# A one-core hybrid encoder layer: bank-emptying operations issued ahead of chain work, and two assumed delays shortened

## The chip, the cores and the metric

The kernel runs on one core of one Trainium2 chip. The metric is the device time of one execution in microseconds, as the median of several runs. Before the change it is 1443.79 us (three runs, 1440.97 to 1444.25). About 0.3% (4.3 us) is what a measurement of this kernel can tell from no change.

## The reference, cut to what matters

One layer, sequence 2048, width 1024, all in float32. A normalised input is projected by one matrix into three head groups; their gated outputs are concatenated and projected back.

```python
hn = rmsnorm(x, norm_g)
z = jnp.einsum('bsd,de->bse', hn, w_in)
(aq, ak, av, ag, mq, mk, mv, mo, mi, mf, mg, gq, gk, gv, ga, gg) = jnp.split(z, split_idx, axis=-1)
att = band_chunk_attention(aq, ak, av, rel_bias)             # 9 chunks of 64 keys, softmax
y_a = att * silu(ag)
qk = silu(causal_conv(concat([mq, mk]), conv_w))
h_ml = mlstm_chunkwise(mq_c, mk_c, mv, mi + b, mf + b)       # matrix memory, carried over chunks
y_b = sigmoid(mo) * head_rmsnorm(h_ml) * silu(mg)
log_alpha = log_sigmoid(ga @ w_alpha + b_alpha) / 16
h_gla = gla_chunkwise(gq, gk, gv, log_alpha)                 # gated linear attention, carried over chunks
y_c = head_rmsnorm(h_gla) * silu(gg)
return x + concat([y_a, y_b, y_c]) @ w_out                   # then a final rmsnorm
```

## The kernel before, in words

**Two phases.** Phase A runs over four blocks of 512 tokens (`q` = 0 to 3). In each block the projections run on PE (TensorE) with the two recurrent groups, mLSTM and gated linear attention (GLA), woven in between. Phase B is attention and the output projection.

**A projection** (`proj_f`, lines 243 to 245) is 24 matmuls of 128x512 into one of two `ip` banks; each operand is split in a high and a low part, and three products are made for each of eight slices. `proj_t` (lines 263 to 265) makes token-major tiles in the same two banks. A *piece* is 12 of these matmuls. A bank is read out by ACT (ScalarE) and DVE (VectorE) operations: for the first token-major projection by `evac1`, whose operations are L411, L413 and L414 (two of the last), for `gq` and `gk` by L431 and L432. The third tile in a row needs the first one's bank empty.

**Order of a block.** `gq`, `gk`, eight token-major tiles, `gg`, the six tiles of the mLSTM's queries and keys, six gate tiles, nine attention tiles (`proj_a`). `gates` runs at the head of the block: two matmuls (L336 and L343) into the single `pw` bank, then a chain of scans and exponentials on ACT and DVE (L272 to L374), each step on what the one before gave. `prep_x` loads the block after it (L285) and squares it on ACT (L286).

**What sets the order.** PE's order is the order in which the program is written. There the class `Flow` keeps a clock of assumed time: every piece and every chain step adds its PE time to it, and a chain is taken up again, behind a piece, once its assumed delay is over. Chains are generators; `yield pe, gap` gives a step's PE time and the delay until its next step. `flow.need("gla_in")` at line 762, after the gate tiles, runs that chain to its end with nothing but other chains' steps in between: here this is called the *drain*. Where assumed time has to jump, it jumps; on the chip PE waits. On the other engines a scheduler orders the operations by its own timeline: of those that it thinks ready, the one with the highest priority goes first. `tc.high_priority(offset=AHEAD)` raises the priority, and does not make an operation ready sooner.

**The chain steps by name.** `gla_in` has, for each half of a block, four groups of GpSimd products (L639 and L642, into four buffers `prd`), each followed by four PE reductions (L648): eight groups to a block. GLA takes three steps a chunk: g.A (L678 to L682), g.B (L699 to L706), g.C (L729). mLSTM takes four: m.A (L521), m.B (L531, L535), m.C (L549 to L566), m.D (L600). Each has one buffer of some bank or tile which the next one needs back. After the last block both chains run to their end with no projection between (the *tail*); four attention projections are kept for phase B.

Of the kernel before, what the change touches and what calls it, by code (L numbers as in the profile page):

```python
# [10 lines left out]
AF = mybir.ActivationFunctionType  # L11
ALU = mybir.AluOpType
# [14 lines left out]
AHEAD = 1500  # L27
# [72 lines left out]
def f32(ap):  # L100
    return ap.bitcast(FP32)
# [3 lines left out]
def trunk_kernel(ctx: ExitStack, tc: tile.TileContext, xT, x, w_f, w_t, w_o, w_gates, norm_g, conv_w,  # L105
# [36 lines left out]
    with ExitStack() as pa_:  # L142
# [113 lines left out]
        def proj_t(j, X, evac):  # L256
            ws = [load_w(w_t[j, g], 2) for g in range(4)]
            for tt in range(NC):
                t = slice(tt * P, (tt + 1) * P)
                ps = bank("ip", 2)  # L260
                for k in range(KT):
                    w = ws[k // 2][:, k % 2]
                    nc.tensor.matmul(ps, X[k][:, 0, t], w[:, 0, :], start=(k == 0), stop=False)  # L263
                    nc.tensor.matmul(ps, X[k][:, 0, t], w[:, 1, :], start=False, stop=False)  # L264
                    nc.tensor.matmul(ps, X[k][:, 1, t], w[:, 0, :], start=False, stop=(k == KT - 1))  # L265
                    if k % 4 == 3:
                        flow.piece(12 * 0.227)
                evac(tt, ps)

        def log_sigmoid(pairs):  # L270
            for dst, src, ab in pairs:
# [120 lines left out]

        def sig_tile(ps):
            th = ev.tile([P, QT], FP32, name="e")
            nc.scalar.activation(th, ps, AF.Tanh, scale=0.5)
            return th

        def silu_tile(ps):
            th = sig_tile(ps)
            nc.vector.scalar_tensor_tensor(th, th, 1.0, ps, op0=ALU.add, op1=ALU.mult)  # L400
            return th

        def proj_v(X):
# [24 lines left out]

        def proj_z(X):
            z = big.tile([P, 2, QT], FP32, name="zg", bufs=1)  # L430
            nc.scalar.activation(z[:, 0, :], proj_f("gq", X), AF.Copy, scale=32.0 ** -0.5)  # L431
            nc.scalar.copy(z[:, 1, :], proj_f("gk", X))  # L432
            return z

        def proj_gg(X):
# [7 lines left out]
        def proj_m(X):  # L443
            qk = big.tile([P, 6, QT], FP32, name="qk", bufs=1)
            tail = big.tile([P, 6, 3], FP32, name="tail")
            for b in range(6):
                ps = proj_f(("mq" if b < 3 else "mk") + str(b % 3), X)
                zb = big.tile([P, 3 + QT], FP32, name="u", bufs=1)
                nc.scalar.copy(zb[:, 3:], ps)
                if st["zb"] is None:  # L450
                    nc.gpsimd.memset(zb[:, 0:3], 0.0)
                else:
                    nc.gpsimd.tensor_copy(zb[:, 0:3], st["zb"][:, b, :])
                nc.gpsimd.tensor_copy(tail[:, b, :], zb[:, QT:QT + 3])
                acc = qk[:, b, :]
                nc.scalar.activation(acc, zb[:, 0:QT], AF.Copy, scale=cw[:, b, 0:1])
                for i in range(1, 4):
                    nc.vector.scalar_tensor_tensor(acc, zb[:, i:i + QT], cw[:, b, i:i + 1], acc, op0=ALU.mult, op1=ALU.add)
                th = ev.tile([P, QT], FP32, name="e")
                nc.scalar.activation(th, acc, AF.Tanh, scale=0.5)  # L460
                nc.vector.scalar_tensor_tensor(acc, th, 1.0, acc, op0=ALU.add, op1=ALU.mult)
            st["zb"] = tail
            return qk
# [10 lines left out]
        def att_in(q, X, b, ps):  # L474
            t0 = q * QT
            if b >= 6:
                th = silu_tile(ps)
                nc.sync.dma_start(ga_d[:, b - 6, t0:t0 + QT], th)
                return
            hl = ev.tile([P, 2, QT], FR, name="hl")  # L480
            scl = 0.125 if b < 3 else 1.0
            nc.scalar.activation(hl[:, 0, :], ps, AF.Copy, scale=scl)
            nc.vector.scalar_tensor_tensor(hl[:, 1, :], ps, scl, f32(hl[:, 0, :]), op0=ALU.mult, op1=ALU.subtract)
            if b < 3:
                nc.sync.dma_start(q_d[b, :, :, t0:t0 + QT].rearrange("l d t -> d l t"), f32(hl))
            else:
                for h in range(2):
                    nc.sync.dma_start(k_d[2 * (b - 3) + h, :, :, t0:t0 + QT].rearrange("l d t -> d l t"),
                                      f32(hl[64 * h:64 * h + 64]))
# [121 lines left out]
        def gla_in(q, z, ls_all, G):  # L611
            NB = ST // 16
            for sub in range(2):
# [23 lines left out]
                for c in range(16):  # L637
# [4 lines left out]
                    nc.gpsimd.tensor_tensor(pc[:, :, 0:c + 1], b16(gk)[:, :, 0:c + 1],  # L642
                                            b16(qq)[:, :, c:c + 1].broadcast_to([P, NB, c + 1]), op=ALU.mult)
                    if c % NP == NP - 1:
                        yield 0.0, 7.0
                        for e in range(c - NP + 1, c + 1):
                            w = 16 if e < 4 else e + 1
                            nc.tensor.matmul(b16(dr_ps[32 * (e % 4):32 * (e % 4) + 32, 0:ST])[:, :, 0:w], hs4[:, e // 4, :],  # L648
                                             b16(prd[:, e % NP, :])[:, :, 0:w], start=(e < 4), stop=(e >= 12), skip_group_check=True)
                        yield 0.35, 0.0  # L650
# [4 lines left out]
        def gla(q, vg, gg, G):  # L655
            for sub in range(2):
# [7 lines left out]
                for c in range(2):  # L664
# [66 lines left out]
                    nc.vector.tensor_tensor(yt, y_ps[:, 0:256].rearrange("p (b t) -> p b t", b=2),  # L731
                                            gg[:, :, sub * ST + c * L:sub * ST + (c + 1) * L], op=ALU.mult)
                    nc.sync.dma_start(y_d[q, :, 6:8, sub * ST + c * L:sub * ST + (c + 1) * L], yt)
                    yield 0.25, 4.0

        nc.sync.dma_start(ng, norm_g)
        R = {}
# [364 lines left out]
```

## Time and profile before

| | |
|---|---|
| median of the runs | 1443.79 us |
| the profiled execution | 1438.14 us, its span 1436.3 us |
| phase A, to the first matmul of attention | about 1015 us |
| PE busy | 1325.9 us, 92% of the span |
| DVE, ACT, POOL (GpSimd) busy | 55%, 42%, 43% |
| mean granted clock of PE | 0.943 |

PE is the busiest engine by far, so a reader looks for the places where it stands still or runs at the lower granted clock, and asks who is waited for there. The other engines' idle time costs nothing by itself. Durations of matmuls overlap: the distance of two starts, about 0.23 us for 128x512 at the full clock, is what one costs. The prediction times a piece, 12 of them, by this: 2.7 us.

### The profile page before, as it was taken

The page shows a single profiled execution, that of the slowest core. Times are in us where ns is not written, and L with a number is a line of the kernel's source. Part 1 is how long each engine was busy: PE and PEld are TensorE (multiplying, and loading weights), DVE is VectorE, ACT ScalarE, POOL GpSimd, SP SyncE. Part 2 cuts the span into 40 slices and gives each one's busy share as a digit, 9 for nine tenths or more (in the row PEclk, how much of TensorE's full clock was granted, in tenths as well). Part 3 has the DMA queues.
Part 4 walks back from the last instruction along what each step waited for, and adds up shares of the span by engine and source line. Part 5 has one row for each costly group of instructions (what it writes and reads, how often), then busy time and mean ns, then how long its engine had stood idle before and what let it go on. Part 6 is the DMA issues. An engine that isn't in the chain of part 4 may idle for free.

```text
span 1436.3 us, 20063 instructions
## 1 busy us (share of the span) xinstructions
PE 1325.9 (92%) x7044; PEld 1073.8 (75%) x7044; DVE 791.9 (55%) x1886; ACT 601.7 (42%) x1149; POOL 621.2 (43%) x847
## 2 busy tenths in 40 slices
PE   5899989989998998999899899997878999999997
PEld 2688867868886786888678677886766887877876
DVE  7626546762654666264466625646556756656731
ACT  5634312463431246343133524332356555655531
POOL 4215662321665222266533415743246354453442
PEclk7999979999997999999799999998987999999999
DMA  7443214554321455432144533331488464655322
GB/s 248 147 131 100 85 39 123 151 176 128 103 74 39 118 153 178 126 107 73 45 119 126 140 120 104 89 112 49 134 215 257 143 182 128 183 155 156 102 69 87
DMA packets 107206, 180.11 MB, mean 125 GB/s; under 512 B 9824, under 2 KB 54752, under 8 KB 107104
## 3 DMA queue, kind: packets, MB, share of 16 engines
q1 hardware_dynamic: 102496, 170.43, 40.1%
q10 hardware_dynamic: 4608, 8.39, 1.6%
q8 instruction: 56, 0.92, 0.3%
q14 instruction: 46, 0.38, 0.1%
HBM read 143.14 MB, written 35.65 MB: 124 GB/s over the span
## 4 chain that ended last, share of the span: by engine, by line
PE 70%; DVE 10%; DMA 6%; POOL 5%; ACT 4%; issue 4%; SPq 1%; POOLq 0%; DVEq 0%; ACTq 0%
PE ip L243 12%; PE ip L245 12%; PE ip L244 12%; PE s L851 3%; PE ip L975 3%; PE ip L973 3%; PE ip L974 3%; PE ip L263 3%; PE ip L264 3%; PE ip L265 2%; PE tp L915 2%; PE ga L682 2%; DVE pt L865 2%; PE s L554 2%; PE w L932 2%
## 5 line engine op out<-in xcount | busy, mean ns | idle before, releaser
L243 PE MATMUL ip<-x,w 128*128 128x512 f32 x800 | 327.5, 409 | 0.0
L245 PE MATMUL ip<-x,w 128*128 128x512 f32 x800 | 314.0, 393 | 0.0
L244 PE MATMUL ip<-x,w 128*128 128x512 f32 x800 | 314.0, 392 | 0.0
L235 ACT CAST w<-wraw 128x1024 fp32r<-128x1024 f32 x132 | 138.3, 1048 | 264.3 <-PE ip L245 189.9
L236 DVE TENSOR_TENSOR w<-wraw,w 128x1024 fp32r<-128x1024 f32 x88 | 115.3, 1310 | 181.1 <-ACT w L235 180.5
L236 POOL TENSOR_TENSOR w<-wraw,w 128x1024 fp32r<-128x1024 f32 x44 | 106.2, 2413 | 205.6 <-ACT w L235 205.5
L243 PEld LDWEIGHTS ip<-x,w 128*128 128x128 f32 x800 | 151.5, 189 | 43.2 <-issue 13.9
L245 PEld LDWEIGHTS ip<-x,w 128*128 128x128 f32 x800 | 151.3, 189 | 33.2
L244 PEld LDWEIGHTS ip<-x,w 128*128 128x128 f32 x800 | 151.8, 190 | 31.2 <-issue 2.4
L870 POOL TENSOR_SCALAR pt<-pt,sm 128x640 f32<-128x640 f32 (+2 forms) x96 | 70.7, 738 | 150.1 <-DVE sm L869 117.6
L263 PE MATMUL ip<-w,x 128*128 128x512 f32 x256 | 105.2, 411 | 23.1 <-DVE hl L414 21.8
L264 PE MATMUL ip<-w,x 128*128 128x512 f32 x256 | 103.5, 404 | 3.5 <-POOL w L236 2.7
L973 PE MATMUL ip<-wo,y 128*128 128x512 f32 x256 | 106.6, 416 | 0.0
L868 ACT ACTIVATE pt<-pt,sm 128x640 f32<-128x640 f32 (+2 forms) x96 | 73.3, 764 | 71.2 <-DVE sm L865 68.6
L265 PE MATMUL ip<-w,x 128*128 128x512 f32 x256 | 103.0, 402 | 0.0
L975 PE MATMUL ip<-wo,y 128*128 128x512 f32 x256 | 101.2, 395 | 0.3 <-POOL y L881 0.3
L974 PE MATMUL ip<-wo,y 128*128 128x512 f32 x256 | 101.2, 395 | 0.0
L642 POOL TENSOR_TENSOR prd<-gk,zg 128x16 f32<-128x16 f32 (+15 forms) x128 | 75.3, 588 | 59.2 <-PE pw L648 53.0
L921 DVE TENSOR_TENSOR pl<-tp,ph 128x512 fp32r<-128x512 f32 (+2 forms) x126 | 74.6, 599 | 32.4 <-ACT ph L920 31.0
L851 PE MATMUL s<-kk,qq 128*128 128x384 f32 (+1 forms) x360 | 80.9, 335 | 10.2 <-DVE sm L865 8.7
L851 PEld LDWEIGHTS s<-kk,qq 128*128 128x128 f32 x360 | 61.0, 202 | 28.7 <-DVE sm L865 21.9
L263 PEld LDWEIGHTS ip<-w,x 128*128 128x128 f32 x256 | 50.2, 196 | 36.4 <-DVE hl L414 23.5
(244 smaller groups left out, 2447.2 us busy)
## 6 DMA issues: line engine op xcount, KB each, us to landing
wraw<-in_w_f SPq DMA_DIRECT2D x100, 512.0 KB, 3.6
wraw<-in_w_t SPq DMA_DIRECT2D x32, 512.0 KB, 4.0
qq<-q_d SPq DMA_DIRECT2D x48, 256.0 KB, 4.5
kk<-k_d SPq DMA_DIRECT2D x18, 512.0 KB, 6.6
vv<-v_d SPq DMA_DIRECT2D x18, 512.0 KB, 7.5
xraw<-in_x SPq DMA_DIRECT2D x16, 512.0 KB, 5.3
xraw<-in_xT SPq DMA_DIRECT2D x16, 512.0 KB, 7.2
xr<-in_x SPq DMA_DIRECT2D x16, 512.0 KB, 4.0
```

The costliest lines, as they stand in the source:

```text
L235: nc.scalar.copy(w[:, :, 0, :], rv)
L236: other().tensor_tensor(w[:, :, 1, :], rv, f32(w[:, :, 0, :]), op=ALU.subtract)
L243: nc.tensor.matmul(ps, w[:, k, 0, :], X[k][:, 0, :], start=(k == 0), stop=False)
L244: nc.tensor.matmul(ps, w[:, k, 0, :], X[k][:, 1, :], start=False, stop=False)
L245: nc.tensor.matmul(ps, w[:, k, 1, :], X[k][:, 0, :], start=False, stop=(k == KT - 1))
L263: nc.tensor.matmul(ps, X[k][:, 0, t], w[:, 0, :], start=(k == 0), stop=False)
L264: nc.tensor.matmul(ps, X[k][:, 0, t], w[:, 1, :], start=False, stop=False)
L265: nc.tensor.matmul(ps, X[k][:, 1, t], w[:, 0, :], start=False, stop=(k == KT - 1))
L851: nc.tensor.matmul(sp[:, :cn], qq[:, l, tt * P:(tt + 1) * P], kk[:, ko + c0:ko + c0 + cn], start=(l == 0), stop=(l == 1))
L973: nc.tensor.matmul(ps, Y[k][:, 0, t], wo[k, j][:, 0, :], start=(e == 0), stop=False)
L974: nc.tensor.matmul(ps, Y[k][:, 0, t], wo[k, j][:, 1, :], start=False, stop=False)
L975: nc.tensor.matmul(ps, Y[k][:, 1, t], wo[k, j][:, 0, :], start=False, stop=(e == KT - 1))
```

## The change

It does two things. First, the operations that empty the projections' banks, on ACT and DVE, get the raised priority that weight loads and the input's split already have: `evac` in `proj_t`, `sig_tile` and `silu_tile`, both evictions of `proj_z`, the one in `proj_m`, and the query and key evictions in `att_in`. Second, two delays that `Flow` assumes for GLA shrink: that of a `gla_in` group from 7.0 to 6.0, and that after the last step of a GLA chunk from 4.0 to 0.5. No operation is added or taken away.

```diff
@@ proj_t
-                evac(tt, ps)
+                with tc.high_priority(offset=AHEAD):
+                    evac(tt, ps)
...
@@ sig_tile, silu_tile
-            nc.scalar.activation(th, ps, AF.Tanh, scale=0.5)
+            with tc.high_priority(offset=AHEAD):
+                nc.scalar.activation(th, ps, AF.Tanh, scale=0.5)
...
-            nc.vector.scalar_tensor_tensor(th, th, 1.0, ps, op0=ALU.add, op1=ALU.mult)
+            with tc.high_priority(offset=AHEAD):
+                nc.vector.scalar_tensor_tensor(th, th, 1.0, ps, op0=ALU.add, op1=ALU.mult)
...
@@ proj_z
-            nc.scalar.activation(z[:, 0, :], proj_f("gq", X), AF.Copy, scale=32.0 ** -0.5)
-            nc.scalar.copy(z[:, 1, :], proj_f("gk", X))
+            pq = proj_f("gq", X)
+            with tc.high_priority(offset=AHEAD):
+                nc.scalar.activation(z[:, 0, :], pq, AF.Copy, scale=32.0 ** -0.5)
+            pk = proj_f("gk", X)
+            with tc.high_priority(offset=AHEAD):
+                nc.scalar.copy(z[:, 1, :], pk)
...
@@ proj_m
-                nc.scalar.copy(zb[:, 3:], ps)
+                with tc.high_priority(offset=AHEAD):
+                    nc.scalar.copy(zb[:, 3:], ps)
...
@@ att_in
-            nc.scalar.activation(hl[:, 0, :], ps, AF.Copy, scale=scl)
-            nc.vector.scalar_tensor_tensor(hl[:, 1, :], ps, scl, f32(hl[:, 0, :]), op0=ALU.mult, op1=ALU.subtract)
+            with tc.high_priority(offset=AHEAD):
+                nc.scalar.activation(hl[:, 0, :], ps, AF.Copy, scale=scl)
+                nc.vector.scalar_tensor_tensor(hl[:, 1, :], ps, scl, f32(hl[:, 0, :]), op0=ALU.mult, op1=ALU.subtract)
...
@@ gla_in
-                        yield 0.0, 7.0
+                        yield 0.0, 6.0
...
@@ gla
-                    yield 0.25, 4.0
+                    yield 0.25, 0.5
```

The orders below are those of the built programs. The changed file has up to nine lines more, so its line numbers run ahead: L657 there is L648 here, L609 is L600, L530 is L521, L738 is L729, L687 to L691 are L678 to L682, L540 and L544 are L531 and L535; L417 is L414, L287 is L286, L341 is L340, L436 is L431, L273 is L272.

**PE, the drain of the first block.** Before, from m.D on:

```order
L600 MATMUL mt<-ident,m 128x128 x3
L521 MATMUL s<-hl_nm,sel 128x128 x6
L729 MATMUL gb<-ident,n 128x128 x2
L648 MATMUL pw<-prd,hs_157 32x16x5
L648 MATMUL pw<-prd,hs_157 32x16x6
L648 MATMUL pw<-prd,hs_157 32x16x7
L648 MATMUL pw<-prd,hs_157 32x16x8
L531 MATMUL s<-qk 128x128 x6
L535 MATMUL mt<-ident,qk 128x128 x3
L678 MATMUL gb<-ident,dr 128x128
L679 MATMUL gb<-ident,kd 128x128
L682 MATMUL ga<-Qb,Kt 128x64 x7
```

Now, from m.D on:

```order
L609 MATMUL mt<-ident,m 128x128 x3
L530 MATMUL s<-hl_nm,sel 128x128 x6
L738 MATMUL gb<-ident,n 128x128 x2
L687 MATMUL gb<-ident,dr 128x128
L688 MATMUL gb<-ident,kd 128x128
L691 MATMUL ga<-Qb,Kt 128x64 x7
L657 MATMUL pw<-prd,hs_157 32x16x9
L657 MATMUL pw<-prd,hs_157 32x16x10
L657 MATMUL pw<-prd,hs_157 32x16x11
L657 MATMUL pw<-prd,hs_157 32x16x12
L540 MATMUL s<-qk 128x128 x6
L544 MATMUL mt<-ident,qk 128x128 x3
```

The group of columns 5 to 8 has moved ahead, to between projections. Behind these rows the drain before still has m.C, the group 9 to 12, g.B and the group 13 to 16; now it has g.B and the group 13 to 16, and m.C comes after a further piece. So two groups are left in the drain where there were three, and no m.C. The drains of the second and third blocks have the same rows.

**ACT, the head of the second block** (L286 squares the next block's input, L340 empties the `pw` bank of the first gate matmul, L272 starts the chain of the gates). Before:

```order
L286 ACTIVATE xraw,rs<-xraw 128x1024 x2
L340 COPY g<-pw 6x512
L286 ACTIVATE xraw,rs<-xraw 128x1024
L235 CAST w<-wraw 128x2x512
L431 ACTIVATE zg<-ip 128x512
L286 ACTIVATE xraw,rs<-xraw 128x1024
L272 ACTIVATE g<-pw 128x512
```

Now:

```order
L287 ACTIVATE xraw,rs<-xraw 128x1024 x3
L341 COPY g<-pw 6x512
L287 ACTIVATE xraw,rs<-xraw 128x1024
L436 ACTIVATE zg<-ip 128x512
L235 CAST w<-wraw 128x2x512
L273 ACTIVATE g<-pw 128x512
```

The copy that frees the `pw` bank stands behind the third of the squares instead of the second, and the bank's eviction and the cast behind the fourth. On PE the second gate matmul (L343, now L344) stands one piece earlier in the second to fourth blocks, with m.D just ahead of it: before, two pieces lie between the two gate matmuls, now one.

**DVE, the same place, up to the second operation that empties the first token-major tile.** Before:

```order
L356 TENSOR_TENSOR g<-g 6x512
L629 TENSOR_TENSOR qt<-zg,qt 128x256
L633 TENSOR_TENSOR Dt<-Dt,dl 128x2
L414 TENSOR_TENSOR hl<-ip,hl 128x3x64
L629 TENSOR_TENSOR qt<-zg,qt 128x256
L633 TENSOR_TENSOR Dt<-Dt,dl 128x2
L628 TENSOR_TENSOR lc<-lc,zg 128x256 x2
L359 TENSOR_TENSOR g<-g 6x512
L633 TENSOR_TENSOR Dt<-Dt,dl 128x2x2 x2
L414 TENSOR_TENSOR hl<-ip,hl 128x3x64
```

Now:

```order
L638 TENSOR_TENSOR qt<-zg,qt 128x256
L642 TENSOR_TENSOR Dt<-Dt,dl 128x2
L642 TENSOR_TENSOR Dt<-Dt,dl 128x2x2
L417 TENSOR_TENSOR hl<-ip,hl 128x3x64
L637 TENSOR_TENSOR lc<-lc,zg 128x256
L362 TENSOR_TENSOR g<-g 6x512
L366 TENSOR_TENSOR rows<-g,ml 6x128
L367 TENSOR_TENSOR rows<-g 6x384
L642 TENSOR_TENSOR Dt<-Dt,dl 128x2x2
L642 TENSOR_TENSOR Dt<-Dt,dl 128x2x3
L364 TENSOR_TENSOR hl_nm<-g,hl_nm 6x512
L417 TENSOR_TENSOR hl<-ip,hl 128x3x64
```

Here L361, L365, L366 and L363 of before (now L362, L366, L367 and L364) have come ahead of the second eviction. In the first block the DVE rows at this place are the same before and now.

## The prediction

> **What bounds the kernel.** I read the page first, for the busiest engine and its clock.
>
> ```profile
> span 1436.3 us, 20063 instructions
> PE   5899989989998998999899899997878999999997
> PEclk7999979999997999999799999998987999999999
> ```
>
> PE is at 90% or more in most slices, so time can come only from PE's waits and from its dips in clock. The dips (7 at slices 5, 12 and 19, some 35.9 us each) come once in each of the first three blocks. Who PE waits for in phase A tells the next view, PE's waits up to 1015 us (total, times, longest):
>
> ```profile
> PE ip L263 <- DVE hl L414: 21.8, 4, 6.4
> PE pw L648 <- POOL prd L642: 14.8, 12, 2.6
> PE mt L600 <- DVE m L591: 11.5, 3, 5.9
> PE mt L535 <- DVE m L602: 3.4, 2, 1.7
> PE ip L263 <- ACT zg L432: 1.3, 2, 0.8
> ```
>
> Evictions hold PE at one place a block only: the third token-major tile, which waits for L414 of the first. No L243 row waits for its bank: the evictions of `gg`, of the gate tiles and of the attention tiles are hidden already, and hurrying them is worth nothing. The second and fourth rows belong to the drain, the third to the tail. Busy time by stretch (us, then busy and count for PE, PEld, DVE, ACT, POOL, then granted clock, DMA share, GB/s) shows how much these places cost, three drains, then two of the four eviction stalls:
>
> ```profile
> 185.50:210.10 24.60, 18.85 (x119) 14.54 (x115) 12.89 (x39) 4.24 (x10) 18.44 (x38) 0.63 0.13 36
> 435.70:461.70 26.00, 19.35 (x119) 15.24 (x115) 11.41 (x37) 4.26 (x10) 19.57 (x38) 0.66 0.13 33
> 687.00:711.60 24.60, 18.85 (x119) 14.54 (x115) 12.86 (x39) 4.26 (x10) 18.42 (x38) 0.63 0.12 36
> 306.10:311.10 5.00, 0.12 (x2) 0.07 (x1) 4.78 (x17) 3.56 (x9) 0.57 (x2) 1.00 0.12 49
> 806.60:813.20 6.60, 0.17 (x2) 0.10 (x1) 6.38 (x20) 5.37 (x15) 3.13 (x7) 0.72 0.01 0
> ```
>
> A drain is 25 us long at a clock of 0.63 to 0.66, with POOL busy for three quarters of it. In an eviction stall DVE is busy throughout: PE waits for DVE to get through chain work.
>
> **Term 1, the drains.** The timeline shows what sets their pace:
>
> ```profile
> 185.59 0.36 POOL L642 TENSOR_TENSOR prd<-gk,zg 128x80 f32<-128x80 f32 x1 [1.46 <-PE pw L648]
> 189.19 0.42 POOL L642 TENSOR_TENSOR prd<-gk,zg 128x128 f32<-128x128 f32 x1
> 189.55 0.41 DVE L731 TENSOR_TENSOR n<-gb,gg 128x256 f32<-128x256 f32 x1
> 189.67 0.41 PE L648 MATMUL pw<-prd,hs 128*32 128x128 f32 x2 [0.61 <-POOL prd L642]
> 190.63 1.26 POOL L471 TENSOR_TENSOR gm<-e 128x512 f32<-128x512 f32 x1
> 201.44 0.87 PE L648 MATMUL pw<-prd,hs 128*32 128x144 f32 x8
> 209.03 1.06 PE L648 MATMUL pw<-prd,hs 128*32 128x256 f32 x2 [2.27 <-POOL prd L642]
> ```
>
> POOL's products of a group need the four buffers back from the group before: they start at 185.59, when PE has read the last group, and end at 189.61, so a group costs POOL 4.0 us undisturbed. PE stands behind them in its order. Between 189.7 and 201.4 PE does m.B, g.A and m.C at half clock, and the last group is waited for again. Now two groups are left, and g.A stands ahead of both. Counted from the drain's start: m.D, m.A and g.C come to about 1.8 us on PE, then g.A waits for L731, which frees bank `gb` behind six L524 (in the row above it ends 3.5 us after g.C began), and is through at about 5.5. Meanwhile POOL does three of the four products of group 9 to 12 and L471 (4.0 + 1.3 = 5.3 us with the fourth); some products of `Kt`, which wait for g.A, stand ahead of that fourth, so it ends at about 6.9 and the group's matmuls at 7.8. The rest of `Kt` (about 1.1 us) and the last group on POOL (4.0 to 4.4, its operands being longer) make 13.3, its last matmuls 1.1 more: 14.5 us. m.B and g.B fit on PE between 7.8 and 13.3 at half clock. The step taken out, m.C, is then paid behind a projection at the full clock, as in this block's later chunk:
>
> ```profile
> 235.54 0.94 PE L549 MATMUL s<-Cbd,qk 128*128 128x130 f32 x6
> 237.70 0.57 PE L566 MATMUL mt<-v,m 128*64 128x65 f32 x12
> ```
>
> which is 2.7 us (235.54 to 238.27), and the group that moved forward 0.6. So a block gains 24.6 - 14.5 - 2.7 - 0.6 = 6.8 us, the second block 8.2, the three together 21.8. Bounds: two POOL groups and one matmul group without a disturbance, 4.0 + 4.0 + 0.9 + 1.1 = 10, plus 1 to hand over, give 11 us and a gain of 32 over three blocks; with groups as slow as the slowest of this block,
>
> ```profile
> 150.27 0.58 POOL L642 TENSOR_TENSOR prd<-gk,zg 128x208 f32<-128x208 f32 x1 [2.63 <-PE pw L648]
> 157.08 0.65 POOL L642 TENSOR_TENSOR prd<-gk,zg 128x256 f32<-128x256 f32 x1
> ```
>
> 7.5 us each (a 1.67 us product and gate work lie between), a drain is some 20 us and the gain 6 in all. The same rows bound the cost of the shorter delay between projections. The tightest pair of groups now has two pieces, m.B and one piece between (5.4 + 1.4 + 2.7 = 9.5 us) against those 7.5, so I cost it at nothing; the cover is 2 us, and beyond that every microsecond of POOL is one of PE, in four blocks.
>
> What the clock does in a drain: in the first one PE has no gap above 2.3 us (the row of 209.03), and yet the granted clock averages 0.63. The Trainium skill ("TensorE: Matmul & The Clock Gate", section "What's actually happening") has the clock halve after an idle window of about 3.4 us and come back after a busy one. By that rule a drain with no wait above 2 us would keep its clock; this trace disagrees, since small matmuls with short waits lost it too.
>
> **Term 2, the head of a block.** The evictions at L414 were to come first. They don't: in the first block DVE's rows there are unchanged, since the scheduler still thinks the chain's operations ready sooner than the bank, and ACT only swaps a cast with an eviction. So the first stall stays. In the second and third blocks the chain's start moves:
>
> ```profile
> 287.69 0.69 DVE L339 COPY g<-pw 6x512 f32<-6x512 f32 x1
> 290.15 1.06 ACT L286 ACTIVATE xraw<-xraw 128x1024 f32<-128x1024 f32 x1 [1.16 <-DMA xraw<-in_x]
> 291.20 1.03 ACT L235 CAST w<-wraw 128x1024 fp32r<-128x1024 f32 x1
> 292.14 0.59 ACT L431 ACTIVATE zg<-ip 128x512 f32<-128x512 f32 x1
> 292.63 1.05 ACT L286 ACTIVATE xraw<-xraw 128x1024 f32<-128x1024 f32 x1
> 293.67 0.58 ACT L272 ACTIVATE g<-pw 128x512 f32<-128x512 f32 x1
> 290.75 1.02 PE L343 MATMUL pw<-g,gsel 128*128 128x512 f32 x2
> ```
>
> L343 needs the one `pw` bank that L339 and L340 read. L340 now stands behind the third square, which waited for its DMA until 290.15; with L340 (0.58) behind it the bank is free at about 291.9, while PE comes to L343 a piece earlier, at 288. So PE waits there 2.5 to 4 us and gains nothing by the earlier place. Behind L340 are queued the fourth square, L431 and L235, and only then L272, where before L431 and L235 had been done while the fourth square's data was on its way: L272 starts 0 to 1.6 us later than at 293.67 (the upper end if the fourth load lands as late as the row of 292.63 allows). Then DVE:
>
> ```profile
> 310.63 0.35 DVE L414 TENSOR_TENSOR hl<-ip,hl 128x192 fp32r<-128x192 f32 x1
> 311.01 0.69 DVE L361 TENSOR_TENSOR g<-g 6x512 f32<-6x512 f32 x1
> 311.83 0.55 DVE L366 TENSOR_TENSOR rows<-g 6x384 f32<-6x384 f32 x1
> 312.68 0.78 DVE L363 TENSOR_TENSOR hl_nm<-g,hl_nm 6x512 fp32r<-6x512 f32 x1
> ```
>
> What ran from 311.01 to 313.46 now runs ahead of that L414, about 2.3 us. The third tile, which sets off from there, is thus 2.3 to 3.9 us later against the block's start if the chain starts no earlier; at best the chain starts as much earlier as DVE adds, and nothing is lost. I take 2.5, and 1.0 for the clock (a second stall at L343), twice; in the fourth block, which has no squares, L339 stands behind L591 instead, and the extra DVE rows are fewer: 1.0. Together 8 us lost, between 0 and 13.
>
> **Term 3, the tail.** Here mLSTM's two last chunks set the end:
>
> ```profile
> 996.85 0.90 PE L600 MATMUL mt<-ident,m 128*128 128x128 f32 x3 [5.92 <-DVE m L591]
> 1013.36 0.90 PE L600 MATMUL mt<-ident,m 128*128 128x128 f32 x3 [4.78 <-DVE m L591]
> ```
>
> One chunk takes 16.5 us from m.D to m.D, whatever GLA does beside it. By the new order a g.A, a g.C and a group have come ahead of the last three chunks' work (some 3 us later), and the g.A between m.B and m.C is gone (1.9 us, twice). Minus 1, give or take 3. Phase B has the same PE order; moved casts and DMA issues there I cost at 0, give or take 2.
>
> **Sum.** -21.8 + 8 - 1 = -15 us: from the profiled execution's 1438.1 to 1423. That execution lies 5.7 us under the median of the runs shown, so the median of the changed kernel should be 1429, for the likeliest case between 1417 and 1439.
>
> **Rivals.**
> - *The evictions do come early.* If the stalls at L414 vanish, 21.8 us go, and some 1.7 of half clock behind each of four: -29 instead of +8, so 1392. For it: DVE is busy throughout the stall, so only order is in the way. Against it: the order shown. Chance 0.06.
> - *The clock stays up in the shorter drain.* At full clock the PE steps in it are shorter by half and the projections behind it start at full clock: about 3 us a block, 1420. For it: two waits fewer. Against it: 0.63 with short waits. Chance 0.10. The rule of the Trainium skill ("TensorE: Matmul & The Clock Gate", section "What's actually happening") gives this outcome.
> - *POOL sets the pace anyway* and the drains stay near 20 us: -6 + 8 - 1, so 1445, no change. For it: POOL is busy 18.4 of 24.6 us, and its work is the same. Against it: that work overlaps with three more pieces now. Chance 0.14.
> - *Slower: the square's DMA at L340.* PE, held at L343, is at the mercy of the third and fourth input loads. This decides once they land 8 us later than before, so that the second and third blocks lose 11 us each and the drains' gain is spent; at 15 us each the time is 1444 - 22 + 30 + 1 - 1 = 1452. For it: each of these loads waits for a buffer that DVE's L329 frees, which shares its time with mLSTM's steps now moved there. Against it: 290.15 was already late. Chance 0.10.
>
> **Chances.** The forecast has 0.60. Faster by over 0.3%, which is 4.3 us and about what a measurement can tell: the forecast (its own range ends at 1439, just faster by that bound) and the first two rivals, 0.76. Within: 0.14. Slower: 0.10. The range has to reach the third rival and leave out the ends: 1412 to 1445.
>
> **What would show it.** Right: the windows of the three drains at 13 to 17 us; the wait of L648 for POOL below 10 us in all; L263 still waiting for L414 four times, 20 us or more; a new wait of L343 for ACT's L340 in the second and third blocks. Wrong: the L414 wait under 10 us, drains above 20 us, or waits of L648 in the midst of projections, in slices where PE is at 9 now.

## The result

The changed kernel takes 1419.56 us (median of four runs, 1417.13 to 1425.18) against 1442.38 us for the kernel before, measured beside it. The ratio is 0.985, with a 95% interval of 0.982 to 0.989: some 21 us, or 1.5%, less. The forecast was 1429, faster. It has the sign and the place right, and it is 9.4 us too high.

The page of the changed kernel, to be held against the same lines of before:

```profile
span 1415.3 us, 20032 instructions
...
PE   4899999989998998999899899997978999999997
...
PEclk7999999999999999999899999997978999999999
```

The three dips of the granted clock at slices 5, 12 and 19 (counted from 0) hardly show any more: 7 before, 9 and once 8 now. What PE waits for up to 1015 us (total, times, longest):

```profile
PE ip L263 <- DVE hl L417: 20.0, 4, 5.2
PE mt L609 <- DVE m L600: 11.7, 4, 5.1
...
PE gb L687 <- DVE n L740: 6.9, 4, 1.8
...
PE pw L657 <- POOL prd L651: 5.2, 5, 2.6
PE pw L344 <- ACT g L341: 1.1, 1, 1.1
...
PE ip L264 <- POOL w L236: 0.8, 1, 0.8
```

The eviction stall (L263 for L417, before L414) is nearly what it was, 20.0 us for 21.8; the 1.5 us of it that are gone are the fourth block's (6.4 before, 4.9 now). The groups' wait for POOL fell from 14.8 to 5.2. The m.D wait (L609, before L600) is as long as before but stands elsewhere: before, it was the tail's alone, now half of it lies in the blocks. The three drains, from the end of the last projection ahead of them to the next one (us, then busy and count for PE, PEld, DVE, ACT, POOL, granted clock, DMA share, GB/s):

```profile
185.87:200.03 14.16, 11.41 (x86) 8.90 (x85) 9.43 (x25) 4.21 (x9) 12.80 (x25) 0.76 0.26 80
429.13:444.82 15.69, 10.84 (x85) 7.49 (x84) 9.15 (x24) 4.21 (x9) 13.75 (x25) 0.78 0.18 54
672.07:686.13 14.06, 11.21 (x85) 8.15 (x84) 9.02 (x25) 4.21 (x9) 12.19 (x24) 0.76 0.25 62
```

They are 14.2, 15.7 and 14.1 us long. The same stretches, from projection to projection, took 25.2, 26.6 and 25.2 us before.

**Where the time went, stage by stage.** Both kernels run the same 3168 projection matmuls in the same order, the four kept tiles among them. So the start of one of them in the one trace, less its start in the other, is the gain so far, wherever the chains stand level:

| stage | us against before |
|---|---|
| to the first drain | +0.2 |
| first drain to the first token-major tile of block 2 | -6.2 |
| that block's token-major tiles | -0.8 |
| the same two stages, block 2 into 3 | -7.1, -1.2 |
| the same, block 3 into 4 | -2.8, -6.9 |
| last block's projections and tail | +1.4 |
| phase B (422.0 to 424.3) | +2.3 |
| span (1436.3 to 1415.3) | -21.0 |

The rows are rounded, so they add up to 0.1 more than the span.

**Waits and half clock.** How much of this is waiting, and how much is slower matmuls? From the first token-major tile of the first block to the last piece ahead of the tail (columns as above; before, then now):

```profile
45.24:978.31 933.07, 887.53 (x4617) 714.01 (x4616) 500.08 (x1033) 350.80 (x598) 410.91 (x606) 0.95 0.36 108
44.58:953.59 909.01, 871.05 (x4624) 699.22 (x4623) 508.83 (x1035) 350.53 (x599) 398.90 (x606) 0.98 0.37 111
```

The matmuls are the same, but for a few at the edges. PE stands idle for 45.5 us before and 38.0 now, 7.5 less. It is also busy for 16.5 us less with the same work. The clock accounts for that to within 2.2 us: the profile's clock records lie at full or at half, and PE was busy at half clock for 74.7 us before and for 37.3 now; half of the difference is 18.7 us. So of the 24.1 us gained in this stretch about a third is waiting, and the larger part is half clock. Busy time less half of the busy time at half clock comes to 850 to 853 us in 13 of the 14 kernels of this document, and to 857 in the one with the delay at 6.0 alone: it is PE's work in this stretch at full clock.

Two of the rows by stage were not foreseen. In the third block the gain is less than half of the others', because m.D waits there. DVE does eight products of the next block's normalisation ahead of the operation that m.D needs:

```profile
696.66 7.33 DVE L308 SCALAR_TENSOR_TENSOR xraw<-xraw,ng,g 128x512 f32<-128x512 f32 x8 [0.73 <-ACT g L301]
703.92 0.41 DVE L740 TENSOR_TENSOR n<-gb,gg 128x256 f32<-128x256 f32 x1
704.25 0.54 DVE L600 TENSOR_TENSOR m<-m,sm 128x384 f32<-128x384 f32 x1
```

PE waited 3.67 us for that L600 at 704.85, and 3.4 us of half clock follow. In the token-major tiles of the fourth block 6.9 us were gained. Before, the granted clock was down there twice (6.8 us each; now once, 3.4 us), and a weight came late; the first two rows are ACT's and PE's of before, the third is ACT's of the changed kernel:

```profile
829.32 1.05 ACT L235 CAST w<-wraw 128x1024 fp32r<-128x1024 f32 x1 [2.13 <-DMA wraw<-in_w_t]
832.87 0.50 PE L264 MATMUL ip<-w,x 128*128 128x512 f32 x1 [1.95 <-POOL w L236]
```

```profile
808.46 1.05 ACT L235 CAST w<-wraw 128x1024 fp32r<-128x1024 f32 x1 [0.96 <-DMA wraw<-in_w_t]
```

The load was issued at 824.18 before and had landed at 829.32, 5.1 us later; now it took 3.7 us (804.78 to 808.46). Behind it PE waited 1.95 us before, with 6.8 us of half clock after it, and not at all now, with none. On SP's queue the last transfer of phase B's inputs was issued 3.2 us ahead of this load before, and 7.0 us ahead of it now. That the two transfers got in each other's way is argued from this, not shown.

### The profile page after: what moved, and what is told of

Same layout as the page of the kernel before. It is cut to its first block, busy times and chain, and to the rows that moved or that the text cites. A ratio compares the mean times of both kernels' runs of the same rounds, so it can differ in the third digit from the quotient of the medians.

```text
span 1415.3 us, 20032 instructions
## 1 busy us (share of the span) xinstructions
PE 1312.1 (93%) x7044; PEld 1062.7 (75%) x7044; DVE 800.6 (57%) x1886; ACT 600.9 (42%) x1149; POOL 608.2 (43%) x847
## 4 chain that ended last, share of the span: by engine, by line
PE 71%; DVE 12%; DMA 5%; POOL 4%; ACT 4%; issue 3%; SPq 1%; POOLq 0%; DVEq 0%; ACTq 0%
PE ip L243 13%; PE ip L245 12%; PE ip L244 12%; PE s L860 3%; PE ip L263 3%; PE ip L264 3%; PE ip L984 3%; PE ip L983 3%; PE ip L982 3%; PE ip L265 3%; PE tp L924 2%; DVE pt L874 2%; PE w L941 2%; DMA wraw<-y_d 1%; PE ga L691 1%
## 5 line engine op out<-in xcount | busy, mean ns | idle before, releaser
L243 PE MATMUL ip<-x,w 128*128 128x512 f32 x800 | 328.5, 411 | 0.0
L244 PE MATMUL ip<-x,w 128*128 128x512 f32 x800 | 313.0, 391 | 0.0
L243 PEld LDWEIGHTS ip<-x,w 128*128 128x128 f32 x800 | 151.1, 189 | 45.5 <-issue 16.1
L244 PEld LDWEIGHTS ip<-x,w 128*128 128x128 f32 x800 | 151.4, 189 | 30.2 <-issue 2.6
L263 PE MATMUL ip<-w,x 128*128 128x512 f32 x256 | 104.5, 408 | 20.0 <-DVE hl L417 20.0
L860 PEld LDWEIGHTS s<-kk,qq 128*128 128x128 f32 x360 | 60.7, 202 | 31.0 <-DVE sm L874 25.2
L929 ACT CAST ph<-tp 128x512 fp32r<-128x512 f32 (+2 forms) x126 | 63.1, 509 | 37.1 <-PE tp L924 36.3
```

The costliest lines, as they stand in the source:

```text
L243: nc.tensor.matmul(ps, w[:, k, 0, :], X[k][:, 0, :], start=(k == 0), stop=False)
L244: nc.tensor.matmul(ps, w[:, k, 0, :], X[k][:, 1, :], start=False, stop=False)
L860: nc.tensor.matmul(sp[:, :cn], qq[:, l, tt * P:(tt + 1) * P], kk[:, ko + c0:ko + c0 + cn], start=(l == 0), stop=(l == 1))
```

## The experiments

All times are medians, each with the ratio to the kernel before that was run beside it.

### Both delays, no raised eviction

```diff
-                        yield 0.0, 7.0
+                        yield 0.0, 6.0
-                    yield 0.25, 4.0
+                    yield 0.25, 0.5
```

> Both delays shortened, no eviction raised. The order on PE is that of the changed kernel. If the gain is the drains' (the prediction's first term), nearly all of it is here: 1416 to 1426 us, the three drains at 14 to 16 us each. If the raised evictions share in the gain (rival), it stays above 1430.

1417.8 us, 0.985 (0.983 to 0.987): the whole gain, with the drains at 14.7, 16.3 and 14.7 us.

### The raised evictions alone

The diff of the document's beginning without those two lines.

> The evictions raised, the delays as before. The order on PE is that of the kernel before. Theory: no PE wait in phase A hangs on a hurried eviction, since L414 stays behind the chain's rows in every block: 1438 to 1448 us, drains at 24 to 26 us, L263 waiting for L417 some 20 us in all. Rival: the raised evictions also set casts and transfers free earlier and bring 5 us or more by themselves.

1438.7 us, 1.000 (0.998 to 1.002). As expected: the wider half of the diff does nothing that can be measured. On ACT and DVE the order in the traces differs at some 400 of 3035 places, yet the drains take 22.9, 27.0 and 25.0 us, and L263 still waits four times for L417, 23.5 us in all.

### The delay of a gla_in group alone

```diff
-                        yield 0.0, 7.0
+                        yield 0.0, 6.0
```

> Only the delay of a gla_in group shortened to 6.0. Two groups are left in the drain as with both delays, but no g.B, and the second gate matmul stands right behind the first, four pieces ahead of the first token-major tile instead of two. Theory: this one delay takes a group and m.C out of the drain, so the drains fall to 13 to 16 us and the gain is the whole 20 to 28 us: 1413 to 1424. The chain starts some 2 pieces earlier too, which can shorten the stalls at L414 of blocks 2 to 4 by up to 5 us each, against a wait of 2 to 4 us of L343 for the one pw bank. Rival: each of the two delays brings about half, 1430 to 1434.

1443.4 us, 1.003 (1.001 to 1.004): not faster at all. Neither the theory nor the rival foresaw this. Its drains:

```profile
185.70:200.20 14.50, 11.75 (x67) 6.93 (x66) 7.88 (x20) 3.83 (x8) 12.00 (x23) 0.73 0.21 61
439.60:455.50 15.90, 11.54 (x67) 7.59 (x66) 6.47 (x19) 3.83 (x8) 13.25 (x24) 0.68 0.18 54
690.80:705.40 14.60, 11.66 (x67) 6.87 (x66) 7.79 (x20) 3.84 (x8) 12.04 (x23) 0.73 0.20 60
```

So this delay alone makes the drains as short as both do, and a projection behind the first drain starts 9.8 us earlier than before. But by the first token-major tile of block 2 the same kernel is 9.6 us behind. What PE waited for between 200 and 300 us says where 10 of these 19.4 us went:

```profile
PE mt L600 <- DVE m L591: 4.4, 1, 4.4
PE pw L343 <- ACT g L340: 4.3, 1, 4.3
PE gb L729 <- DVE n L724: 1.3, 1, 1.3
```

In the same stretch the kernel with both delays has one wait, 1.9 us for L591. m.C and g.B, paid behind the drain (204.20 to 208.54), are 4.4 us more, and PE works 11.1 us at half clock in this stretch, against 2.1 before, which costs 4.5. No projection stands between the two gate matmuls here, and the second waits 11.8 us in three blocks for its bank. The stall at L414 is gone in blocks 2 to 4, since the gates' chain starts two pieces earlier: only the first block's 5.7 us is left. It doesn't pay for the rest.

### The delay after a GLA chunk alone

```diff
-                    yield 0.25, 4.0
+                    yield 0.25, 0.5
```

> Only the delay after the last step of a GLA chunk shortened to 0.5. Three groups stay in the drain. Theory: POOL's three groups set its length, so the drains stay at 21 to 26 us and the time at 1436 to 1446 us. Rival: g.A earlier is what shortens the drain, and the time falls by 10 us or more.

1442.6 us, 1.003 (1.001 to 1.005). Three groups stay in the drains, and these stay long (28.3, 25.5, 25.2 us); the first:

```profile
185.40:213.70 28.30, 21.06 (x124) 15.02 (x122) 13.84 (x40) 4.75 (x10) 18.79 (x38) 0.57 0.10 32
```

So neither delay alone makes the kernel faster (ratios 1.003 and 1.003), and the two together bring some 21 us. The 6.0 shortens the drains; the 0.5 adds nothing to that. But with both, GLA's steps stand elsewhere in PE's order, and between the first drain and block 2's first token-major tile PE waits 1.9 us instead of 10.0 and does nothing at half clock: only so is the drain's gain kept.

### The gates four pieces earlier

From here on the base is the changed kernel. `proj_a` calls what it is handed ahead of the attention tile of that number, counted from 0.

```diff
+            def early_gates():
+                flow.need("prep")
+                flow.start("gates", gates(q + 1, R["g1"], R))
-            proj_a(q, X)
+            proj_a(q, X, (7, early_gates) if q + 1 < NQ else None)
             if q + 1 < NQ:
-                flow.need("prep")
                 X = split_x(R["raws"])
-                flow.start("gates", gates(q + 1, R["g1"], R))
```

> The changed kernel with the gates of the next block started two attention tiles (four pieces) earlier; in blocks 2 to 4 all of their chain's DVE rows then stand ahead of the first token-major tile, and no row stands between its two L417. Theory (the prediction's): each eviction stall is DVE getting through the gates' chain, so the three stalls of blocks 2 to 4 (4.9 us each, with some 1.5 us of half clock behind each) vanish and only the first block's 5 us stays: 1396 to 1406 us, if L344 does not wait over 2 us a block for L341. Rival: the stall moves into mLSTM's steps, whose DVE rows now share the time with the gates' chain (L609 waiting 3 us more in each block), and the time stays at 1414 or above.

1418.3 us, 0.984 (0.982 to 0.986): no better. The cause of the stall was right, the gain not:

```profile
PE mt L611 <- DVE m L602: 27.0, 6, 8.2
...
PE ip L263 <- DVE hl L417: 5.3, 1, 5.3
```

The three eviction stalls are gone, 14.7 us, and the m.D wait (L611 is L609 of the changed kernel) is 15.3 us longer. In this order it is m.D's DVE rows that stand behind the gates' chain.

### Less work for POOL in the drain

```diff
-                nc.gpsimd.tensor_tensor(gm[:, a, :], th, sl, op=ALU.mult)
+                (nc.vector if a == 2 else nc.gpsimd).tensor_tensor(gm[:, a, :], th, sl, op=ALU.mult)
...
+                    eng = nc.vector if sub == 1 and c >= 14 else nc.gpsimd
...
```

Both products of a column go to `eng`.

> The changed kernel with GpSimd's share of the drain made smaller: the last gate product of a block (1.29 us) and the last two columns' products of a block's second half (2.7 us) run on DVE instead. Theory: POOL sets the length of the drain, so each drain (14.1, 15.7, 14.1 us from the last projection's end to the next) is 3 to 4 us shorter and the time falls by 9 to 12 us, to 1406 to 1412. Rival: PE's own steps at the lower granted clock set it, and the drains stay within 1 us of what they were.

1415.5 us, 0.982 (0.981 to 0.984).

```profile
184.88:198.27 13.39, 9.76 (x85) 7.40 (x84) 9.79 (x28) 4.21 (x9) 8.73 (x18) 0.87 0.28 83
428.00:443.10 15.10, 11.50 (x84) 8.73 (x78) 10.69 (x29) 4.26 (x10) 10.50 (x20) 0.77 0.22 56
671.00:684.90 13.90, 11.52 (x77) 8.79 (x76) 10.59 (x30) 3.98 (x9) 9.17 (x20) 0.68 0.25 64
```

POOL is busy 8.7 us of the first drain instead of 12.8, and the drain is 0.8 us shorter (0.6 and 0.2 in the others): the theory's 3 to 4 us didn't come. In the first of these drains the clock was down for 3.4 us, in the changed kernel for 6.8, so that alone doesn't set the length either. What changed is who is waited for. g.A (L687 there, L688 here) now waits 2.4 us for DVE instead of 1.7, and the last group waits 1.3 us for a product on DVE. But the run loads DVE with what it takes off POOL. That other chains of nearly the same length run beside POOL's is therefore argued from these rows, not shown.

### The preparation two pieces later

```diff
                 R = {}
-                flow.start("prep", prep(q + 1, R, dg))
-            proj_a(q, X)
+                dgx, Rx = dg, R
+                def late_prep(q=q):
+                    flow.start("prep", prep(q + 1, Rx, dgx))
+            proj_a(q, X, {1: late_prep} if q + 1 < NQ else None)
```

> The changed kernel with the preparation of the next block started one attention tile (two pieces) later, so that the eight DVE products of the normalisation stand behind the L600 of the third m.D instead of ahead of it. Theory: the wait of that m.D in the third block (3.67 us, and 3.4 us of half clock behind it) goes: 3 to 6 us less, 1414 to 1417. Rival: the eight products (7.3 us) then hold the next step that DVE feeds, in all three blocks, and the time rises by 3 us or more.

1411.2 us, 0.980 (0.977 to 0.982), 8 us below the changed kernel and more than expected. The m.D of the third block waits no more, and between 686 and 728 us (times of the changed kernel) 7.5 us are gained on it there. But this gain isn't kept: m.D waits 2.2 us at the head of the fourth block instead, and by that block's first token-major tile the lead is 1.5 us, where it was 1.9 at the drain. m.D's waits are 11.8 us in all, as in the changed kernel; L417 is waited for 15.4 us instead of 20.0. Of the 8.8 us between the two profiled spans 4.9 lie in phase B, which this edit leaves as it is. So the theory's wait went away as expected, and why the kernel is faster stays open.

### Both of these

> Both of these: gates four pieces earlier, preparation two pieces later. If both causes are as in the theory, the gains add: 1391 to 1402 us. If one of the two only moves its wait, it stands no better than the gates alone.

1413.7 us, 0.981 (0.979 to 0.982): no better than the later preparation alone. The eviction stall is again the first block's only, and m.D waits in the tail alone. In their place PE waits for the split of the next input, 8.4 us of L243 for ACT's L329 and 4.0 of L244 for L330.

### The drain two pieces later, the preparation four

```diff
-                flow.need("gla_in")
                 R = {}
-                flow.start("prep", prep(q + 1, R, dg))
-            proj_a(q, X)
...
+            proj_a(q, X, {1: lambda: flow.need("gla_in"), 2: late_prep} if q + 1 < NQ else None)
```

> The changed kernel with the drain put two pieces later (behind the first attention tile) and the preparation of the next block four pieces later (behind the second), so that m.D and g.C stand among projections and only m.A, g.A, m.B, g.B and two groups in the drain. Theory: a drain's 14 us hold some 7.5 us of PE work at the full clock (m.D to the last group), and the rest is waiting for DVE and POOL; two pieces (5.4 us) between take up the wait for L740 and POOL's group: each drain 3 to 5 us shorter, 10 to 15 us in all against the kernel with the later preparation (1411.2), so 1396 to 1404 us. Rival: the work behind the drain (the next block's preparation, its gates) comes so late that L344, L609 and L417 wait more, and the time stays at 1408 or above.

1412.4 us, 0.983 (0.981 to 0.984). A rival's result: the time stays. By the 62nd piece the first drain has given 3.9 us more than in the changed kernel, and at the head of the block m.D takes it back, waiting 8.3 us. Over phase A:

```profile
PE mt L611 <- DVE m L602: 27.4, 5, 8.3
...
PE ip L263 <- DVE hl L417: 6.4, 2, 5.4
```

### The drain four pieces later, the preparation six

The same with 2 and 3 in place of 1 and 2.

> The same with the drain four pieces later and the preparation six pieces later; nothing but g.B, m.C and one group is left of the drain. The two matmuls of the gates then stand next to each other, four pieces ahead of the first token-major tile. Theory: the drains fall below 6 us each (20 us less in all than with both delays alone), but the second gate matmul waits some 4 us a block for L341, as it did with the one delay at 6.0 (11.8 us over three blocks): 1395 to 1406 us. Rival: what the delay at 6.0 alone lost at the head of a block (some 15 us each) is lost here too, 1420 or above.

1424.8 us, 0.991 (0.989 to 0.992), above the changed kernel's 0.985 (0.982 to 0.989), as the rival said. The gate matmuls stand next to each other, and L344 waits 18.2 us in three blocks for L341, m.D 31.3 us for L602.

### The last m.D of a block behind the gates' chain

On the kernel with the drain two pieces later:

```diff
-                yield 1.7, 9.0
+                yield 1.7, 18.0 if c == NC - 1 and q < NQ - 1 else 9.0
```

> The kernel with the drain two pieces and the preparation four pieces later, and besides the assumed delay ahead of the last m.D of a block (not of the last block) at 18 instead of 9, which puts it behind four pieces of the first token-major tiles instead of right ahead of them. Theory: that m.D waited (8.3, 7.8 and 3.6 us) because DVE has L602, which it needs, behind the gates' chain; nobody waits for m.D itself, so placed after that chain it waits for nothing, and 15 to 22 us go: 1390 to 1398 us. Rival: the token-major tiles then wait for L417 behind the same chain, 4 us or more a block, and the time stays at 1403 or above.

1411.2 us, 0.979 (0.976 to 0.982). m.D waits no more in the blocks, and the evictions wait again, as the rival said:

```profile
PE ip L263 <- DVE hl L417: 16.9, 4, 5.5
...
PE mt L611 <- DVE m L602: 6.3, 2, 5.1
```

### The front of gla_in on POOL

On the kernel with the later preparation: five DVE statements behind gla_in's scan run on POOL. Two of them:

```diff
-                nc.vector.tensor_copy(dl, qt.rearrange("p (c b i) -> p c b i", c=2, i=16)[:, :, :, 15])
+                nc.gpsimd.tensor_copy(dl, qt.rearrange("p (c b i) -> p c b i", c=2, i=16)[:, :, :, 15])
...
-                    nc.vector.tensor_tensor(Dt[:, :, i, 0:i], Dt[:, :, i - 1, 0:i],
+                    nc.gpsimd.tensor_tensor(Dt[:, :, i, 0:i], Dt[:, :, i - 1, 0:i],
```

> The kernel with the preparation two pieces later (1411.2 us), and besides the front of gla_in (the products that follow its scan, L635 to L642 in the changed kernel) moved from DVE to POOL, which stands idle at the head of a block. No operation is taken out. Theory: a stall at the head of a block is DVE's backlog (the gates' chain, gla_in's front and the evictions all want it at once), and moving rows only chose who waits; some 4 us of DVE work a block taken away shortens the four stalls at L417 (15.4 us in all) and the m.D waits ahead of them by 2 to 4 us a block, half clock included: 1397 to 1406 us. Rival: the backlog is not what decides, and the waits turn to POOL's slower products: 1410 or above.

1418.0 us, 0.986 (0.984 to 0.988), 7 us slower than its base. L417 is waited for 18.1 us, 8.1 of them in the first block. Two groups of the gates' chain show that the DVE rows that were left took longer (count, then total us and mean ns of one); with the later preparation alone:

```profile
L360 DVE TENSOR_TENSOR g<-g 6x512 f32<-6x512 f32 x4 | 2.8, 689 | 0.1
L357 DVE TENSOR_TENSOR g<-g 6x512 f32<-6x512 f32 x4 | 2.7, 680 | 0.0
```

and with POOL at work beside them:

```profile
L357 DVE TENSOR_TENSOR g<-g 6x512 f32<-6x512 f32 x4 | 4.4, 1095 | 0.0
L360 DVE TENSOR_TENSOR g<-g 6x512 f32<-6x512 f32 x4 | 4.1, 1031 | 0.1
```

The same operations on DVE take half as long again and more. The Trainium skill ("Perfetto Trace Analysis", section "Optimizing Scalar/DVE Operations") warns that DVE and GpSimd share a read port of the SBUF, so that moving operations between these two might not help; this run agrees, with 0.68 us before and 1.10 beside POOL.

**The head of a block in all of these.** PE's waits for DVE's two users there, up to 1015 us, and for the stretch from the first token-major tile to the last piece ahead of the tail, PE's idle time, its busy time at half clock and the length (all us, one execution each):

| kernel | L417 | m.D | both | idle | half clock | length |
|---|---|---|---|---|---|---|
| changed | 20.0 | 11.7 | 31.7 | 38.0 | 37.3 | 909.0 |
| gates earlier | 5.3 | 27.0 | 32.3 | 41.4 | 39.2 | 913.8 |
| preparation later | 15.4 | 11.8 | 27.2 | 36.1 | 34.7 | 906.6 |
| gates earlier, preparation later | 5.3 | 8.0 | 13.3 | 31.7 | 40.6 | 905.2 |
| drain later | 6.4 | 27.4 | 33.8 | 41.9 | 22.3 | 903.4 |
| drain four pieces later | 5.2 | 31.3 | 36.5 | 50.9 | 31.4 | 916.2 |
| drain later, last m.D later | 16.9 | 6.3 | 23.2 | 36.7 | 31.1 | 903.9 |
| gla_in's front on POOL | 18.1 | 11.1 | 29.2 | 39.9 | 41.1 | 912.6 |

Some 5 to 8 us of each m.D figure are the tail's. The order of PE's steps chooses who waits. The two users' sum doesn't give the time: it is lowest where PE waits for the split of the input instead, and high in the shortest stretch of all, the later drain, where PE works only 22.3 us at half clock. 851 us for the work itself, all of PE's idle time and half of its time at half clock add up to each length to within 3 us.

## Why the prediction was right, and where it was not

**The drains (term 1): the size was right, the reason only in part.** Forecast were 14.5 us each, measured 14.2, 15.7 and 14.1. The first block's gain, with the 1.7 us that m.D waits at the next head counted apart, is 7.9 us for the 6.8 forecast; with the L344 wait (1.1) and the third block's m.D wait and half clock (3.7 + 1.7) counted apart, the other two gave 8.2 and 8.2 for 8.2 and 6.8. Together -24.3 instead of -21.8. The walk along POOL's groups came out: the last product ends 13.5 us after the drain's start, for 13.3, and the last group waits for it. But the walk doesn't say where most of the gain lies. From the piece ahead of the first drain to block 2's first token-major tile PE is idle for 1.4 us less than before (5.8 to 4.4), and busy at half clock for 10.4 us less (17.2 to 6.8), which is worth 5.2. In the changed drains the granted clock was down for 6.8 us each instead of 17 to 18, and the first piece behind them ran at full speed. Why it was down for so much less stays open: no run here shortens the drain and leaves the clock as it was, or the other way round.

The rows of the first drain, PE's, show the waits that it foresaw, for L740 and for the last group, with g.A at half clock between them:

```profile
189.44 0.35 PE L687 MATMUL gb<-ident,dr 128*128 128x128 f32 x1 [1.71 <-DVE n L740]
...
189.79 3.09 PE L691 MATMUL ga<-Qb,Kt 128*128 128x64 f32 x14
192.81 1.00 PE L657 MATMUL pw<-prd,hs 128*32 128x144 f32 x8
...
199.48 0.62 PE L657 MATMUL pw<-prd,hs 128*32 128x256 f32 x2 [1.04 <-POOL prd L651]
```

**The head of a block (term 2) is the step that failed**, by size: +8 was forecast, between 0 and 13; the new waits cost 2.9 us, and with the tiles behind them (-8.9) the term comes to -6.0. Most of that is not the term's: the fourth block's late weight and the half clock behind it (1.95 + 3.4) were left out of the forecast. Without them the term comes to about -0.6, no loss at all. That the evictions would not come earlier held: four stalls, 20.0 us. That L343 would wait for the square's DMA held as a mechanism, with 1.1 us, once. ACT's rows there show why:

```profile
278.89 1.06 ACT L287 ACTIVATE xraw<-xraw 128x1024 f32<-128x1024 f32 x1 [2.14 <-DMA xraw<-in_x]
...
280.15 1.06 ACT L287 ACTIVATE xraw<-xraw 128x1024 f32<-128x1024 f32 x1
...
281.33 0.57 ACT L341 COPY g<-pw 6x512 f32<-6x512 f32 x1
282.12 1.06 ACT L287 ACTIVATE xraw<-xraw 128x1024 f32<-128x1024 f32 x1 [0.22 <-DMA xraw<-in_x]
...
284.59 0.59 ACT L273 ACTIVATE g<-pw 128x512 f32<-128x512 f32 x1
```

The prediction kept the loads' landing where it was against PE's steps (290.15, 4.2 us ahead of the first token-major tile). They land earlier: the fourth square, which L273 stands behind, starts at 282.12 after a wait of 0.22 us, 6.3 us ahead of that tile (288.37), where before it started 1.7 us ahead (292.63), and the third starts 8.2 us ahead. So the chain starts 3.8 us ahead of the tile instead of 0.7, and this pays for the 2.3 us of DVE rows that now run ahead of the second L417. This was the lower bound of the term ("at best the chain starts as much earlier as DVE adds, and nothing is lost"); 2.5 us a block was the wrong choice between the two ends. In block 2 PE did wait at that place, for m.D's L600 (1.73 us, to 281.41). L341 ended at 281.90, just before PE came to L344 at 281.96: without m.D's wait L344 would have waited instead, so the mechanism is there, and smaller than the 2.5 to 4 us that were forecast.

**What it left out** is L600 behind the eight products in the third block (+5.4 us), the fourth block's late weight (5.4 of the -6.9), and the part of half clock in the drains. The tail was +1.4 instead of -1. Phase B's +2.3 is within what other kernels with the same order of PE there show in one execution each (417.6 to 424.9 us), so it is not put down to the change.

**The offset.** Of the 9.4 us by which 1429 is too high, 4 are none of the terms': the profiled execution of before was taken to lie 5.7 us under its median, but the median of 25 further runs is 1439.8, 1.7 above it. Made against the profiled execution, the sum was 1423, and the profiled execution of the changed kernel took 1417.1.

**The rivals.** POOL's pace, no change: its bound of 20 us a drain didn't come about. The clock staying up, at 1420, has the measured time and half of the mechanism: the projections behind the drain did start at full clock, but in each drain it was still down for 6.8 us. That the time agrees to 0.4 us is luck, since in that sum the head of the block still loses 8 us. The square's DMA at L340 needed the loads to land later, and they landed earlier; with the delay at 6.0 alone something of it is real: L343 waits 3.2 to 4.3 us a block, and in block 2 L340 stands behind a square that waited 1.85 us for its load. That the delays and not the raised evictions bring the gain is shown by the first two runs. That they bring it only together was not foreseen. Luck has a part in the forecast, too: the third block's m.D (+5.4) and the fourth block's weight (-5.4), both left out, cancel.

**Lower than both kernels** are the later preparation (0.980, 0.977 to 0.982) and the last m.D put off with the later drain (0.979, 0.976 to 0.982), against 0.985 (0.982 to 0.989) for the change as it was made. They were not run beside the changed kernel, and the intervals touch.

## What to carry to other kernels

A stage that gets shorter hands its time to the next one only if nothing there is late: the delay that shortened the drains by 11 us each gained nothing alone, because m.D and the gates waited instead and the clock fell there. When an engine's queue is full at one place, as DVE's is at the head of a block, moving PE's steps chooses who waits (L417, m.D or the split of the input); add up all of PE's idle time and half of its time at half clock, not one wait or two. And a raised priority need not change anything that is waited for: here it changed the order at some 400 places and took away no stall.

## What the runs showed of the hardware that was not expected

- Elementwise rows on DVE of 6x512 took 0.68 us with POOL mostly idle and 1.03 to 1.10 us on average with POOL at work on a row of products beside them. Beside a single POOL product that began just after it, a DVE row kept its time (0.69 us at 299.63 in the changed kernel), and it was POOL's product that took longer: 0.71 us (299.68) for one that takes 0.33 undisturbed (298.73 with the later preparation).
- The granted clock fell in the changed kernel's drains for 6.8 us with no wait of PE above 1.71 us in the first and third, and PE was busy for 11.4 of the 14.2 us. The rule of the Trainium skill ("TensorE: Matmul & The Clock Gate", section "What's actually happening"), that it takes an idle window of about 3.4 us, does not account for that by PE's waits alone; the stretches of low clock are whole multiples of 3.4 us long (3.4, 6.8, 10.2, 17.1 and 20.5), which fits a window of that length.
- In the first drain of the kernel before, the clock stayed at half from 191.7 to 212.1 us, although PE ran its small matmuls without a wait from 192.6 to 206.8.
